# Column order of x2 in a transformer block's expert stage: contiguous chunks, and a straight gather for the second group

## The chip, the cores and the metric

The kernel runs on one core of a Trainium2 chip. The metric is the device time of one execution in microseconds. Of the kernel before three runs are known: 765.41 us in the median, 764.91 and 768.2 at the ends. All durations come from one further execution, taken by the hardware profiler.

## The reference, cut to what matters

An encoder block on 512 tokens of width 1024: attention of two kinds with one output projection into the residual stream, then a mixture of experts. The residual stream after attention is called x2 here. What the change touches:

```python
h2 = rms_norm(x, g_ffn[l])
pg = softmax(hf @ wg + bg); gsel = argmax(pg)            # one of 4 expert groups
p_top, e_loc = top_k(softmax(le[gsel]), 2)               # two of its 8 experts
gate = pg_sel[:, None] * p_top / sum(p_top)
ys = (silu(xb @ w1[e]) * (xb @ w3[e])) @ w2[e]           # each expert on its tokens
out[tok] += gate * ys                                    # x + out is returned
```

There are 32 experts; w1 and w3 are 1024 x 512 and w2 is 512 x 1024 for each, all in float32. Each token goes to two experts.

## The kernel before, in words

The first 260 us are attention and its output projection. Then x2 lies in SBUF (`xs`) as four tiles of 128 tokens (t = 0 to 3) by 1024 columns, worked on in two halves h of 512 columns.

**Router.** `half_turn` (line 800 on) transposes a half of a token tile by four TensorE transposes of 128 x 128 (line 808) into a bank of PSUM, and ACT copies it (`x2T`). `logits` multiplies it by the router's rows. DVE picks group and experts (`route`), TensorE counts tokens per expert (`count`), DVE makes the place of each token in its expert (`rank`) and, by `match` (line 919), a one-hot matrix that takes a token to a slot.

**Columns.** The contraction over 1024 columns runs in chunks of 128. Before, chunk r of half h is every fourth column, beginning with column r: column 4p + r of the half stands at partition p. Thus row p of the w1 and w3 loads is four neighbouring rows of the matrix, 8 KB in one piece, and x2 is read with a step of four elements. The router's rows and the gains g_ffn (`gfp`) follow the same order.

**Groups.** The experts are worked on in 13 groups, of two experts with 64 slots each or of four with 32 each. The order is (0,2), (2,2), (20,4), (4,2) and so on: first expert and number. For each group x2's rows are brought to the slots, transposed, in one of two ways:

- group 0: `gather_part` (line 922) multiplies x2 itself, as the stationary operand in float32, by the one-hot matrix: four matmuls (line 928) for each half and token tile, which give the transposed rows at once, in the two PSUM banks `px` (tag `tr`). One of these float32 matmuls stands in the trace as two records.
- groups 1 to 12: `prepare` (lines 1158 and 1159) splits a quarter of a half tile into two exact parts (`part`), a high one by a cast on ACT and the rest by a subtraction on DVE; `quarter` (line 1166) multiplies both by the one-hot matrix, 16 quarters a group; ACT copies the result (`st`, line 1172) and `turn` transposes it (line 1178).

`take` (line 1186) then scales by g_ffn on DVE. `finish` (line 1196) makes the turned one-hot matrix and the gates of a group. `hidden` (line 1224) multiplies the gathered rows by w1 and w3, `swish` and `gated` join them, `turn_hidden` (line 1263) transposes, `outputs` (line 1280) multiplies by w2, and `combine` (lines 1324 to 1326) adds the results back into `sums`.

**Order.** It is written out by hand. Group i's `hidden` has 16 steps; in step n, behind its matmuls, the functions in `during[n]` are issued: the previous group's `combine`, and the gathering of group i + 1. `outputs` has eight steps with `after[n]`, in which the gathering of group i + 2 begins. Group 0 is special: in its steps the experts are named (1), the places turned (3), its own last two gather parts done (4), the places sorted and group 1 begun (7); from step 8 on group 1's 16 quarters are issued, two a step, with a turn in step 13 and one behind the last step, and in step 11 group 0's `finish`.

**Loads.** Weights come in pieces of 1 MB on SP's queue (line 715), in the order of use, into a ring of tiles (`bt`, `qs`, `kl`, `kh`, `e`, `n`, `ma`, `mb`, `w_h`, `w_l`). A tile is loaded again when its last reader is done, and SP issues in order.

Of the kernel before, what the change touches and what calls it, by code (L numbers as in the profile page):

```python
# [22 lines left out]
P = 128  # L23
SEQ = 512
D = 1024
NT = SEQ // P
KC = D // P
NE = 32
HID = 512
# [53 lines left out]
def run(*gens):  # L83

    gens = list(gens)
    while gens:
        for g in list(gens):
            try:
                next(g)
            except StopIteration:  # L90
                gens.remove(g)
# [3 lines left out]
def tile_block(ctx: ExitStack, tc: tile.TileContext, a: dict, out: bass.AP):  # L95
    nc = tc.nc
# [6 lines left out]
    def bank(tag, shape=(P, 512), name=None):  # L103
        return psum.tile(list(shape), F32, tag=tag, name=name or f"ps_{tag}")
# [103 lines left out]
    ident = const.tile([P, P], F32, name="ident")  # L208
# [437 lines left out]
    for i, (g, n, j) in enumerate(ORDER):  # L646
        r = res[g, j]
# [1 line left out]
        wv.add(with_split(i, gen))  # L649


    w1 = a["w1"][0].rearrange("e (h p r) f -> e h p (r f)", h=2, p=P)
    w3 = a["w3"][0].rearrange("e (h p r) f -> e h p (r f)", h=2, p=P)
    w2 = a["w2"].rearrange("e c p q j d -> e c p (q j d)")
    NP = NE // 2

# [73 lines left out]
    x_tile = []  # L730
# [27 lines left out]
    gfp = const.tile([P, 2, 4], F32, name="gfp")  # L758
# [5 lines left out]
    iota_s = const.tile([P, SLOTS], F32, name="iota_s")  # L764

    def router_loads():
        nc.sync.dma_start(gfp, a["g_ffn"][0].rearrange("(h p r) -> p h r", h=2, p=P))
        raw_r = pool_at.tile([P, KC, 64], F32, tag="qn", name="raw_r", bufs=2)
        parts = {"w_router_g": raw_r[:, 0:1, 0:32], "w_router_e": raw_r[:, 1:5]}
        for n, r in (("w_router_g", 4), ("w_router_e", 32)):  # L770
            parts[n] = parts[n].rearrange("p a b -> p (a b)").rearrange("p (h c) -> p h c", h=2)
            nc.sync.dma_start(parts[n], a[n][0].rearrange("(h p r) c -> p h (r c)", h=2, p=P))
        for src, c0, n in ((a["b_router_g"], 0, 4), (a["b_router_e"], 4, 32)):
            nc.sync.dma_start(rbias[:, c0:c0 + n], bass.AP(tensor=src.tensor, offset=src.offset, ap=[[0, P], [1, n]]))
        nc.gpsimd.iota(desc, pattern=[[-1, 4]], base=4, channel_multiplier=0, allow_small_or_imprecise_dtypes=True)
        nc.gpsimd.iota(iota_s, pattern=[[1, SLOTS]], base=1, channel_multiplier=0,
                       allow_small_or_imprecise_dtypes=True)
        nc.gpsimd.iota(iota_e, pattern=[[1, NE]], base=0, channel_multiplier=0, allow_small_or_imprecise_dtypes=True)
        nc.gpsimd.affine_select(before, ones_f, pattern=[[1, P]], compare_op=ALU.is_gt, fill=0.0,
                                base=0, channel_multiplier=-1)  # L780
        nc.gpsimd.memset(ones_b, 1.0)
        nc.gpsimd.iota(favour, pattern=[[-1, NE]], base=NE - 1, channel_multiplier=0,
                       allow_small_or_imprecise_dtypes=True)
        nc.gpsimd.iota(favour[:, 0:FIXED], pattern=[[-1, FIXED]], base=FIXED, channel_multiplier=0,
                       allow_small_or_imprecise_dtypes=True)
        nc.gpsimd.tensor_scalar(favour[:, 0:FIXED], favour[:, 0:FIXED], 1e6, None, op0=ALU.mult)
        nc.gpsimd.iota(ids, pattern=[[0, 1]], base=0, channel_multiplier=1, allow_small_or_imprecise_dtypes=True)

        def gains():
            for n, c0, w in (("w_router_g", 0, 4), ("w_router_e", 4, 32)):  # L790
                nc.vector.tensor_tensor(wr[:, :, c0:c0 + w], parts[n].rearrange("p h (r c) -> p (h r) c", r=4),
                                        gfp.rearrange("p h r -> p (h r)").unsqueeze(2).to_broadcast([P, KC, w]),
                                        op=ALU.mult)

        wv.chain((12, gains))
# [6 lines left out]
    def half_turn(t, h, tag="tr"):  # L802

        xh = x_tile[0][:, t, h * 512:(h + 1) * 512]
        pb = bank(tag)
        xp = xh.rearrange("p (b r) -> p r b", r=4)
        for r in range(4):
            nc.tensor.transpose(pb[:, r * P:(r + 1) * P], xp[:, r], ident)
        x2T[2 * t + h] = pool_raw.tile([P, 4, P], F32, tag="w_raw", name="x2T", bufs=4)
        nc.scalar.copy(x2T[2 * t + h], pb.rearrange("p (k t) -> p k t", k=4))  # L810

# [110 lines left out]
    def gather_part(px, oh, h, ts_):  # L922

        for t in ts_:
            x2 = x_tile[0][:, t, h * 512:(h + 1) * 512].rearrange("p (b r) -> p r b", r=4)
            one = oh[:, t].rearrange("p e s -> p (e s)").bitcast(F32)
            for r in range(4):
                nc.tensor.matmul(px[h][:, r], lhsT=x2[:, r], rhs=one, start=(t == NT - 1 and r == 0),
                                 stop=(t == 0 and r == 3), skip_group_check=True)
# [206 lines left out]
    def dispatch(oh, p, px=None):  # L1136
# [6 lines left out]
        d = {"px": px, "parts": rows}  # L1143
# [8 lines left out]
        def prepare(n):  # L1152

            h, t, q = n // 8, NT - 1 - n // 2 % NT, n % 2
            part = d[n] = wk("part", [P, 2, 256], F32R, bufs=2)
            whole = x_tile[0][:, t, h * 512:(h + 1) * 512].rearrange("p (b r) -> p r b", r=4)[:, 2 * q:2 * q + 2]
            hi, lo = (part[:, m].rearrange("p (r b) -> p r b", r=2) for m in range(2))
            nc.scalar.copy(hi, whole)  # L1158
            nc.vector.tensor_tensor(lo, whole, hi.bitcast(F32), op=ALU.subtract)  # L1159

# [220 lines left out]
    def group_dispatch(i, oh=None, px=None):  # L1381
        first, n = groups[i]
        if oh is None:
            oh = one_hot((rank if first < FIXED else rank_s)[:, :, first:first + n], i == 1)
        return dispatch(oh, first // 2, px)

    d = group_dispatch(0, oh0, px)
# [5 lines left out]
    PAUSE = 7  # L1393

    def begin(i):
        d = following[i] = group_dispatch(i)
        d["prepare"](0), d["prepare"](1)

    def call(i, name, *args):
        following[i][name](*args)  # L1400
# [1 line left out]
    for i in range(NG):  # L1402
        last = i == NG - 1
        if i == 1:
            rounds = nc.values_load(cint[0:1, 0:1], min_val=0, max_val=7)
        if not last:
            rest = ahead if i == 0 else load_parts(i + 1)
            for nxt in islice(rest, 1) if i == PAUSE else rest:
                pass
        during, after = [[] for _ in range(16)], [[] for _ in range(8)]  # L1410
        if i == 0:
            def first_gather(d=d):
                d["gather"](1, (1, 0))
                d["take"](1)

            during[1] = [name_experts]
            during[3] = [turn_places]
            during[4] = [first_gather]
            during[7] = [sort_places, partial(begin, 1)]
            during[11] = [lambda d=d: run(d["finish"]("tr"))]  # L1420
        else:
            for n in range(8):
                at_ = (3 if n < 4 else 7) if last else 3 + n // 2 if i == PAUSE else 4 + n // 2 * 2
                during[at_].append(partial(combine, *prev, n // 4, (n % 4,), i == 1))
        if not last:
            if i == PAUSE:
                during[7] += [overflow, lambda: list(rest), partial(begin, i + 1)]
                work_on = [(8 + n // 2, "quarter", n) for n in range(16)] + [(13, "turn")]
            elif i + 1 in following and i:
                work_on = [(n // 2 * 2 - 4, "quarter", n) for n in range(4, 16)] + [(6, "turn")]  # L1430
            elif i:
                begin(i + 1)
                work_on = [(n * 12 // 16 + 2, "quarter", n) for n in range(16)] + [(10, "turn")]
            else:
                work_on = [(8 + n // 2, "quarter", n) for n in range(16)] + [(13, "turn")]
            for n, *what in work_on:
                during[n].append(partial(call, i + 1, *what))
        sl = hidden(i, tiles, d, during)
        if not last:
            call(i + 1, "turn")  # L1440
        ht = turn_hidden(sl, iter(()) if last else following[i + 1]["finish"]("o"))
        if last:
            break
        nd = following[i + 1]
        nd["take"](0), nd["take"](1)
        if i + 2 < NG and i + 1 != PAUSE:
            after[0].append(partial(begin, i + 2))
            for n in range(4):
                after[4 + n // 2 * 2].append(partial(call, i + 2, "quarter", n, "mm"))
        prev = outputs(tiles, ht, d, after), d["oht"]  # L1450
        tiles, d = nxt, following[i + 1]
# [85 lines left out]
```

## Time and profile before

| | |
|---|---|
| median of three runs | 765.41 us |
| profiled execution | 766.24 us |
| its span in the trace | 764.4 us |
| PE (TensorE) busy | 733.8 us, 96% |
| PEld (its weight loads) busy | 457.7 us, 60% |
| DVE busy | 440.3 us, 58% |
| ACT busy | 360.0 us, 47% |
| bytes moved | 228.84 MB, 299 GB/s in the mean |

The profiled execution's time exceeds its span by 1.84 us, which lies around the span. An engine's share of busy time is an average over stages with different limits: what a stage costs is read from that stage. Matmuls are pipelined, and the end of each is modelled, so the durations of neighbouring records overlap, and the pace of a series is read from its starts.

### The profile page before, as it was taken

How to read it: one execution, taken by the hardware profiler on the slowest of the kernel's cores; microseconds unless marked ns; L12 is line 12 of the kernel's file. 1: busy time of each engine (PE TensorE's matmuls, PEld its weight loads, DVE VectorE, ACT ScalarE, POOL GpSimd, SP SyncE). 2: the span in 40 equal slices, each digit the busy share in tenths (PEclk: the TensorE clock that was granted, in tenths of full speed). 3: DMA queues.
4: the chain of work that ended last, by engine and by line, in shares of the span. 5: the costliest groups of instructions: out<-in, count | busy, mean ns of one | idle time of the engine just before them, and what ended most of it. 6: DMA issues, size and time to landing. Idle time of an engine off the chain costs nothing. (4 is left out here: it accounts for less than half of the span.)

```text
span 764.4 us, 13043 instructions
## 1 busy us (share of the span) xinstructions
PE 733.8 (96%) x4748; PEld 457.7 (60%) x4748; DVE 440.3 (58%) x932; ACT 360.0 (47%) x725; POOL 91.8 (12%) x175
## 2 busy tenths in 40 slices
PE   9999999999999999899999999999789999999976
PEld 8899988977889895454444444443234444444223
DVE  4677778776765452565655656563455565565303
ACT  6575867877654421643543434341254344353000
POOL 0302100566663110000000000000000000000000
PEclk9999999999999999999999999999899999999999
DMA  8533111313664955557999999999999999999996
GB/s 312 161 113 91 56 56 55 126 42 111 197 254 172 409 232 208 198 216 316 419 421 420 422 421 419 422 421 419 418 421 421 421 420 420 423 421 420 416 409 258
DMA packets 45902, 228.84 MB, mean 299 GB/s; under 512 B 6885, under 2 KB 9189, under 8 KB 22921
## 3 DMA queue, kind: packets, MB, share of 16 engines
q1 hardware_dynamic: 45688, 227.96, 75.1%
q8 instruction: 38, 0.62, 0.3%
q14 instruction: 32, 0.25, 0.1%
q10 hardware_dynamic: 144, 0.00, 0.0%
HBM read 225.83 MB, written 2.11 MB: 298 GB/s over the span
## 5 line engine op out<-in xcount | busy, mean ns | idle before, releaser
L1158 ACT CAST part<-xs 128x256 fp32r<-128x256 f32 x192 | 119.9, 674 | 121.7 <-PE ps_mm L1166 43.0
L1159 DVE TENSOR_TENSOR part<-xs,part 128x256 fp32r<-128x256 f32 x192 | 115.9, 635 | 58.2 <-ACT part L1158 54.7
L1326 DVE TENSOR_TENSOR sums<-ps_o,sums 128x512 f32<-128x512 f32 x88 | 56.7, 686 | 45.7 <-PE ps_o L1325 45.7
L313 PE MATMUL ps_mm<-w_h,hTl 128*128 128x256 f32 x240 | 69.5, 290 | 0.2
L1224 PE MATMUL ps_mm<-qs,xt 128*64 128x512 f32 (+1 forms) x136 | 68.4, 615 | 1.1 <-DMA qs<-in_w 1.1
L313 PE MATMUL ps_mm<-w_h,hTh 128*128 128x256 f32 x240 | 67.3, 281 | 0.0
L313 PE MATMUL ps_mm<-w_l,hTh 128*128 128x256 f32 x240 | 67.3, 280 | 0.0
L1224 PE MATMUL ps_mm<-mb,xt 128*64 128x512 f32 (+1 forms) x120 | 59.8, 616 | 4.4 <-PEq L1341 4.4
L1224 PE MATMUL ps_mm<-kl,xt 128*64 128x512 f32 (+1 forms) x120 | 60.3, 616 | 0.0
L1224 PE MATMUL ps_mm<-kh,xt 128*64 128x512 f32 (+1 forms) x104 | 50.8, 601 | 0.2 <-DMA kh<-in_w 0.2
L1224 PE MATMUL ps_mm<-w_l,xt 128*64 128x512 f32 (+1 forms) x128 | 50.7, 602 | 0.0
L1224 PE MATMUL ps_mm<-w_h,xt 128*64 128x512 f32 (+1 forms) x120 | 46.8, 601 | 0.0
L313 PEld LDWEIGHTS ps_mm<-w_h,hTl 128*128 128x128 f32 x240 | 45.2, 189 | 1.1 <-DVE hTl L239 0.8
L180 DVE TENSOR_TENSOR w_l<-w_raw,w_h 128x512 fp32r<-128x512 f32 x64 | 44.4, 708 | 1.6 <-ACT w_h L177 1.4
L313 PEld LDWEIGHTS ps_mm<-w_l,hTh 128*128 128x128 f32 x240 | 45.3, 189 | 0.1
L313 PEld LDWEIGHTS ps_mm<-w_h,hTh 128*128 128x128 f32 x240 | 45.2, 188 | 0.0
L518 DVE TENSOR_TENSOR_SCAN p<-p,ones_f 128x513 f32<-128x513 f32 (+3 forms) x32 | 27.5, 859 | 30.6 <-POOL p L513 30.5
L1324 PE MATMUL ps_o<-yl,oht 128*128 128x512 f32 x96 | 43.2, 450 | 0.6 <-DVE sums L1326 0.6
L1253 DVE SCALAR_TENSOR_TENSOR sl<-ps_mm,rsl,sl 128x256 f32<-128x256 f32 x26 | 11.4, 479 | 54.9 <-PE ps_mm L1224 54.9
L1324 PEld LDWEIGHTS ps_o<-yl,oht 128*128 128x128 f32 x96 | 17.9, 187 | 41.8 <-DVE part L1159 24.4
L1267 ACT COPY sl<-ps_mm 128x256 f32<-128x256 f32 x26 | 10.0, 386 | 68.7 <-PE ps_mm L1263 68.7
L177 ACT CAST w_h<-w_raw 128x512 fp32r<-128x512 f32 x64 | 38.2, 621 | 5.2 <-DMA w_raw<-in_w_in 4.9
(299 smaller groups left out, 1781.2 us busy)
## 6 DMA issues: line engine op xcount, KB each, us to landing
qs<-in_w SPq DMA_DIRECT2D x22, 1024.0 KB, 19.8
e<-in_w SPq DMA_DIRECT2D x22, 1024.0 KB, 19.8
kl<-in_w SPq DMA_DIRECT2D x21, 1024.0 KB, 19.8
kh<-in_w SPq DMA_DIRECT2D x21, 1024.0 KB, 19.8
n<-in_w SPq DMA_DIRECT2D x20, 1024.0 KB, 19.8
mb<-in_w SPq DMA_DIRECT2D x20, 1024.0 KB, 19.8
w_h<-in_w SPq DMA_DIRECT2D x20, 1024.0 KB, 19.8
w_l<-in_w SPq DMA_DIRECT2D x20, 1024.0 KB, 19.8
```

Source lines behind the costliest of these rows:

```text
L177: nc.scalar.copy(part(wh, n), raw[i, n])
L180: eng.tensor_tensor(part(wl, n), raw[i, n], part(wh, n).bitcast(F32), op=ALU.subtract)
L313: nc.tensor.matmul(pb[:, u], lhsT=x(t0 + u, k), rhs=y[:, k], start=first, stop=last, skip_group_check=True)
L518: nc.vector.tensor_tensor_scan(rev, rev, ones_f[:, 0:1].to_broadcast([P, n + 1]), 1.0, op0=ALU.mult, op1=ALU.mult)
L1158: nc.scalar.copy(hi, whole)
L1159: nc.vector.tensor_tensor(lo, whole, hi.bitcast(F32), op=ALU.subtract)
L1224: nc.tensor.matmul(ph[n][part], lhsT=d["xt"][h][:, r, part], rhs=w, start=(h == 0 and r == 0), stop=(h == 1 and r == 3))
L1253: nc.vector.scalar_tensor_tensor(s, ph["w3"][:, c], d["rsl"], s, op0=ALU.mult, op1=ALU.mult)
L1267: nc.scalar.copy(s, pb)
L1324: nc.tensor.matmul(pc, lhsT=oht[:, t], rhs=yl[:, c], start=True, stop=False)
L1326: nc.vector.tensor_tensor(sums[0][:, t, cs], pc, (xs if first else sums[0])[:, t, cs], op=ALU.add)
```

## The change

The columns of a half are cut into four contiguous chunks of 128: chunk r of half h is columns 128r to 128r + 127 of it. The host lays out w1, w3, the router's rows and g_ffn to suit, so that the rows of a load remain in one piece for each partition; `half_turn`, `gather_part` and `prepare` read x2 contiguously. Group 1 is now gathered as group 0 is, by eight calls of `gather_part` in steps 8 to 15 of group 0, one a step; it has no `prepare`, `quarter` or `turn`. Its two `px` banks have the tag `tr`, and group 0's `finish` moves from `tr` to the tag `o`. Groups 2 to 12 keep the quarters.

```diff
-    w1 = a["w1"][0].rearrange("e (h p r) f -> e h p (r f)", h=2, p=P)
-    w3 = a["w3"][0].rearrange("e (h p r) f -> e h p (r f)", h=2, p=P)
+    w1, w3 = (a[n].rearrange("e h p r f -> e h p (r f)") for n in ("w1", "w3"))
...
-        nc.sync.dma_start(gfp, a["g_ffn"][0].rearrange("(h p r) -> p h r", h=2, p=P))
+        nc.sync.dma_start(gfp, a["g_ffn"])
...
-            nc.sync.dma_start(parts[n], a[n][0].rearrange("(h p r) c -> p h (r c)", h=2, p=P))
+            nc.sync.dma_start(parts[n], a[n].rearrange("p h r c -> p h (r c)"))
...
-        xp = xh.rearrange("p (b r) -> p r b", r=4)
         for r in range(4):
-            nc.tensor.transpose(pb[:, r * P:(r + 1) * P], xp[:, r], ident)
+            nc.tensor.transpose(pb[:, r * P:(r + 1) * P], xh[:, r * P:(r + 1) * P], ident)
...
-            x2 = x_tile[0][:, t, h * 512:(h + 1) * 512].rearrange("p (b r) -> p r b", r=4)
+            x2 = x_tile[0][:, t, h * 512:(h + 1) * 512].rearrange("p (r b) -> p r b", r=4)
...
-            whole = x_tile[0][:, t, h * 512:(h + 1) * 512].rearrange("p (b r) -> p r b", r=4)[:, 2 * q:2 * q + 2]
-            hi, lo = (part[:, m].rearrange("p (r b) -> p r b", r=2) for m in range(2))
+            whole = x_tile[0][:, t, h * 512 + q * 256:h * 512 + q * 256 + 256]
+            hi, lo = part[:, 0], part[:, 1]
...
     def begin(i):
         d = following[i] = group_dispatch(i)
-        d["prepare"](0), d["prepare"](1)
+        if i > 1:
+            d["prepare"](0), d["prepare"](1)
...
-            during[11] = [lambda d=d: run(d["finish"]("tr"))]
+            during[11] = [lambda d=d: run(d["finish"]("o"))]
...
-                work_on = [(8 + n // 2, "quarter", n) for n in range(16)] + [(13, "turn")]
+                work_on = [(8 + n, "gather", n // 4, (NT - 1 - n % 4,)) for n in range(8)]
...
-        if not last:
+        if not last and i:
             call(i + 1, "turn")
...
+    for n in ("w1", "w3"):
+        data[n] = np.ascontiguousarray(data[n][0].reshape(NE, 2, 4, P, HID).transpose(0, 1, 3, 2, 4))
+    for n in ("w_router_g", "w_router_e"):
+        data[n] = np.ascontiguousarray(data[n][0].reshape(2, 4, P, -1).transpose(2, 0, 1, 3))
+    data["g_ffn"] = np.ascontiguousarray(data["g_ffn"][0].reshape(2, 4, P).transpose(2, 0, 1))
```

## Rows read from the trace of the kernel before

**Rows 1.** Stages: window and length; busy time (instructions) by engine; PEclk, DMA share, GB/s.

```profile
275.30:287.66 12.36, 11.80 (x59) 11.63 (x60) 4.52 (x33) 0.31 (x2) 2.63 (x8) 1.00 0.44 173
287.66:302.14 14.48, 14.48 (x76) 8.44 (x77) 2.68 (x17) 1.05 (x2) 0.00 (x0) 1.00 0.44 155
302.14:324.00 21.86, 17.86 (x85) 8.44 (x84) 11.86 (x26) 13.93 (x26) 0.00 (x0) 1.00 0.58 223
324.00:356.00 32.00, 32.00 (x161) 15.39 (x161) 19.00 (x37) 13.72 (x25) 0.00 (x0) 1.00 0.60 235
356.00:755.00 399.00, 384.31 (x2108) 166.55 (x2107) 214.02 (x416) 149.33 (x273) 0.00 (x0) 0.99 1.01 418
```

**Rows 2.** The chain that ended last: start, length, what.

```profile
744.87 10.08 DMA qs<-in_w
```

**Rows 3.** Waits of the load queue, 280 to 362 us: total, times, longest.

```profile
SPq L715 <- PE ps_mm L1224: 49.0, 7, 11.9
```

**Rows 4.** Weight loads by source line: duration ns min/median/max, first and last start.

```profile
L928 PEld LDWEIGHTS ps_tr<-oh,xs x64: 308/329/332, 275.3 to 297.1; 128*128 128x128 f32 x64
...
L220 PEld LDWEIGHTS ps_sc<-ones_f x6: 190/192/192, 737.8 to 738.4; 128*128 128x128 f32 x6
...
L808 PEld LDWEIGHTS ps_tr<-ident,xs x24: 195/209/218, 260.7 to 271.4; 128*128 128x128 f32 x24
...
L1178 PEld LDWEIGHTS ps_tr<-ident,st x96: 138/140/143, 317.1 to 701.3; 128*128 128x128 f32 x96
```

**Rows 5.** TensorE's timeline, 275 to 298 us.

```profile
275.35 5.84 PE L928 MATMUL ps_tr<-oh,xs 128*128 128x128 f32 x24 [0.29 <-DVE oh L919]
281.02 0.20 PE L909 MATMUL ps_o<-act,ones_b 128*128 128x32 bf16 x2
...
281.30 5.84 PE L928 MATMUL ps_tr<-oh,xs 128*128 128x128 f32 x24
287.66 0.64 PE L1224 MATMUL ps_mm<-bt,xt 128*64 128x512 f32 x1 [0.52 <-DVE xt L1186]
...
293.59 4.00 PE L928 MATMUL ps_tr<-oh,xs 128*128 128x128 f32 x16
```

**Rows 6.** TensorE's timeline, contiguous f32 matmuls: start, length of the series, count.

```profile
92.47 0.88 PE L607 MATMUL ps_o<-v,pT 128*128 128x128 f32 x6
...
737.95 0.83 PE L220 MATMUL ps_sc<-ones_f 128*128 128x128 f32 x6
```

**Rows 7.** DVE's timeline: act, the second one-hot, group 1's one-hot.

```profile
277.54 0.41 DVE L882 SCALAR_TENSOR_TENSOR act<-iota_e,idx,a 128x32 bf16<-128x32 f32 x2
...
281.75 0.43 DVE L919 TENSOR_TENSOR oh<-rank,iota_s 128x256 fp32r<-128x256 f32 x1
...
303.05 0.69 DVE L919 TENSOR_TENSOR oht<-rank,iota_s 128x512 fp32r<-128x512 f32 x1
```

**Rows 8.** POOL's timeline: its last instruction on the router's tiles.

```profile
284.51 0.34 POOL L1067 TENSOR_TENSOR book<-rstd,book 128x64 fp32r<-128x64 f32 x1
```

**Rows 9.** TensorE's groups, 302.14 to 324 us: busy, mean ns, idle before.

```profile
L1166 PE MATMUL ps_sc<-part,oht 128*128 128x256 f32 x32 | 7.4, 324 | 3.3 <-DVE part L1159 3.2
...
L1178 PE MATMUL ps_tr<-ident,st 128*128 128x128 f32 x8 | 1.3, 279 | 0.7 <-ACT st L1172 0.7
```

**Rows 10.** TensorE's timeline in the same stage: its first step, a late pair, an undelayed one.

```profile
302.14 1.08 PE L1224 MATMUL ps_mm<-e,xt 128*64 128x512 f32 x4
304.31 1.02 PE L1166 MATMUL ps_sc<-part,oht 128*128 128x256 f32 x4 [1.09 <-DVE part L1159]
...
318.77 0.74 PE L1166 MATMUL ps_sc<-part,oht 128*128 128x256 f32 x4
319.44 0.64 PE L1224 MATMUL ps_mm<-qs,xt 128*64 128x512 f32 x1
```

**Rows 11.** Page, part 5: busy, mean ns, idle before.

```profile
L1158 ACT CAST part<-xs 128x256 fp32r<-128x256 f32 x192 | 119.9, 674 | 121.7 <-PE ps_mm L1166 43.0
...
L1267 ACT COPY sl<-ps_mm 128x256 f32<-128x256 f32 x26 | 10.0, 386 | 68.7 <-PE ps_mm L1263 68.7
```

## The prediction

> **What bounds the kernel now.** I read the stages first [rows 1]. From 356 us to 755 us the DMA share is 1.01 and the rate 418 GB/s: the expert weights stream without a gap, and TensorE, though 384 of 399 us busy, only follows. Between 275 and 356 us the share is 0.44, 0.44, 0.58 and 0.60, because the weight tiles form a ring and a tile is loaded again only when the matmul that reads it is done. The chain of waits ends as this suggests: its last long piece is a weight transfer, landing at 754.95 [rows 2]. The queue's own waits [rows 3] name what holds the loads back in 280 to 362 us: hidden products of TensorE, 49.0 us in 7 waits. So the stream is fixed in length (the bytes stay the same) and its start follows TensorE's order of work through groups 0 and 1. A microsecond that TensorE gains between the last router work (260 us) and the first hidden step of group 2 (after 356 us) starts the full stream a microsecond earlier and ends the run a microsecond earlier. What ACT or DVE gain behind 356 us is worth nothing, as the transfers cover it.
>
> **What the new column order changes for a matmul.** Before, x2 is the stationary operand with a step of four elements. The loads of 128 columns [rows 4] take 329 ns in the gather (L928) against 192 ns for a contiguous f32 operand of the same shape (L220), and 209 against 140 ns in transposes (L808, L1178). The gather is limited by this: PEld is busy 11.63 of 12.36 us in its stage [rows 1], and 24 records take 5.84 us, 0.243 us each [rows 5]. A contiguous f32 matmul of 128 by 128 by 128 goes at (0.83-0.275)/5 = 0.111 us (L220) or (0.88-0.275)/5 = 0.121 us (L607) a record, 0.275 being the last one's own length [rows 6]. I take 0.115, so each record gains 0.128 us; the bounds are 0.111 and, if the step is not the cause, 0.243. One gather part (one token tile, one half) is four matmuls of two records each: eight records, 1.94 us now and 0.92 us after.
>
> A rule of the Trainium skill speaks against this: "TensorE: Matmul & The Clock Gate", section "LDWEIGHTS (loading the stationary operand)", gives the load by its column count alone (columns over 1.2, in ns), whatever the layout. By it no record would get shorter, which is the slower case below; the loads in rows 4 have 128 columns each and still differ, so the trace does not agree.
>
> **Transposes before the router.** There are 32 transposes of x2. Those that the critical path sees are the 16 of token tiles 3 and 2, ahead of their logits. With 69 ns less per load [rows 4] they give between 0 (load hidden) and 1.1 us; I take 0.4. The other 16 lie beside DVE's routing of tiles 3 and 2, so they give nothing.
>
> **Group 0's gather: before its first hidden product.** Now: three parts from 275.35, the counts from 281.02, then one part and the last two from 281.30 to 287.14, the scaling by DVE, the first hidden product at 287.66 [rows 5]. After: the first three parts take 24 x 0.115 = 2.76 us and end 277.7 (with the 0.4 above). The counts need DVE's act, written by 277.95 now [rows 7], 277.55 then, so they start at once where they now wait for TensorE. The second one-hot was ready at 282.18, 1.16 us after the counts [rows 7]; after, it is ready at 278.9, when the part that covers it ends. Two more parts, 1.84 us, and the same 0.5 us for the scaling give 281.3. Gain: 48 x 0.128 = 6.1, less 0.1 for the wait on act: 6.0 us. A possible new wait is here. POOL's last instruction on the router's tiles ends at 284.85 [rows 8], 3.8 us behind the counts, so at 281.5 after; if DVE's scaled tile takes over memory that POOL still reads, it waits 0 to 0.8 us, and behind it every hidden product. I take 0 and keep 0.8 for the range.
>
> **Group 0's last two parts.** They lie between hidden products from 293.59 [rows 5]: 16 x 0.128 = 2.0 us.
>
> **Group 1: quarters out, straight gather in.** This is the stage 302.14 to 324.00 us, in which TensorE is busy 17.86 of 21.86 us [rows 1]. Removed: 4.0 us of idle time, which is almost all waits of the quarter products for DVE's halves (3.2) and of the turns for ACT (0.7) [rows 9]; 8 pairs of quarters, at least 0.67 us each by the starts of a pair that waits for nothing [rows 10], 5.4, and at most the 7.4 us busy; two turns of four transposes, at most 1.3 and some 0.8 us. So 10.2 to 12.7 us; I take 11.5, since most pairs also wait inside. Added: eight parts, 64 x 0.115 = 7.4 us, and one wait. The gather needs the one-hot of group 1, which DVE writes from 303.05 for 0.69 us [rows 7]; TensorE's step begins at 302.14 and is done at 303.22, so it waits some 0.5 us (0 to the 1.09 until 304.31 that it waits there now [rows 10]), and behind it stand all hidden steps of group 0. Net 11.5 - 7.4 - 0.5 = 3.6 us; with the ends of the pace too, 1.4 and 5.6.
>
> Edits that I cost at nothing. Group 0's finish moves to the other pair of banks, last read by ACT and DVE at the sorting, some 8 us before it is written. The banks that the new gather takes were emptied by DVE before that sorting. The 16 casts and subtractions dropped free ACT and DVE, which nobody waits for then, and the table load of the activation no longer stands in a queue of casts. In later groups a cast of 128 by 256 takes 674 ns; a contiguous copy of that size takes 386 [rows 11]. That is up to 0.29 us in each of 176 casts, some 50 us of ACT, and the like on DVE, all under the stream. Without that cover it would save TensorE its waits for halves, which after 324 us are near nil (32.00 of 32.00 busy) [rows 1]. The w1 and w3 transfers keep their 8 KB per partition in one piece and their order. The six small router loads go out by 202 us and are used after 260; a microsecond more or less on SP is covered.
>
> **The sum.** 0.4 + 6.0 + 2.0 + 3.6 = 12.0 us. Against the profiled execution's own 766.24 us (span 764.4 and 1.84 around it) that is 754.2; against the median of 765.41, 753.4. I put down 753.8. What is late next: the stream itself, saturated from about 344 us, with TensorE's work on groups 1 and 2 unchanged behind it.
>
> **The rivals.**
> 1. *The pace does not follow the layout* (slower). If a record of f32 gather stays at 0.243 us, group 0 gains nothing and group 1 pays 64 x 0.243 = 15.6 + 0.5 for the 11.5 removed: 4.6 us slower, 770.0 us by the median. The place is the eight new parts between group 0's hidden products. It decides from the record pace at which 128 records in all cost what is saved: (64 x 0.243 + 11.5 + 0.4 - 0.6)/128 = 0.21 us. For it: the added matmuls are f32 and two records each, where quarters were one. Against it: rows 4 and 6.
> 2. *Only group 0 gains.* The halves' waits are replaced by others of the same size (the one-hot, a bank, POOL's 0.8), so that group 1's swap gives 0 to 1: 765.4 - 8 + 1 = 758 to 759. For it: 0.5 us of DVE's work is already late there. Against it: ACT and DVE lose 32 instructions of 0.6 us in this stage.
> 3. *Hidden anyway.* If the full stream does not start earlier, since some load of group 2 is held by something that does not move, the end stays at 765 to 766. For it: DMA is at 1.01 in half of the run. Against it: shares under 0.6 before 356 and waits that name TensorE.
>
> **How the numbers follow.** Forecast 0.74 (its own range 750.3 to 757.1: with every term at its better end 1.1 + 6.3 + 2.1 + 5.6 = 15.1 us, at its poorer end 0 + 5.0 + 1.9 + 1.4 = 8.3, from the median); rival 2 0.13; rival 3 0.06; rival 1 0.05; more than the best ends 0.02. The range 750.5 to 760 leaves out rivals 1 and 3 and little else. About 0.5%, 3.8 us, is what this kernel's measurement can tell from none: faster 0.89 (forecast, rival 2, more), the same 0.06, slower 0.05.
>
> **What would show it.** The loads of L928 at about 190 ns and 0.11 to 0.12 us a record; 128 of these records instead of 64; the first hidden product at about 281.3 us; TensorE's wait for L1159 gone before group 0's output products, and those starting at about 312; the share at 1.01 from about 344 to 743. The prediction is wrong if the gather's records stay near 0.24 us, if group 0's output products start later than 316, or if the stream starts at 344 and then shows gaps.

## The result, and the profile after

The changed kernel takes 754.62 us in the median of four runs (754.32 to 755.27), the kernel before 766.36 in four runs beside them: a ratio of 0.9847, 95% interval 0.9821 to 0.9872. The forecast was 753.8 us, with a range of 750.5 to 760. The profiled execution took 755.27 us with a span of 753.6, so 10.8 us of span went; by the medians it is 11.7.

The stages of the changed kernel, as in [rows 1]: window and length; busy time (instructions) of PE, PEld, DVE, ACT, POOL; granted clock, DMA share, GB/s.

```profile
275.18:281.71 6.53, 6.01 (x60) 5.81 (x60) 4.49 (x33) 0.31 (x2) 2.57 (x8) 1.00 0.63 261
281.71:294.24 12.53, 12.53 (x77) 6.49 (x77) 2.68 (x17) 1.05 (x2) 0.04 (x1) 1.00 0.65 222
294.24:313.12 18.88, 18.31 (x109) 10.67 (x108) 2.81 (x10) 3.53 (x8) 0.00 (x0) 1.00 0.59 224
313.12:345.10 31.98, 31.98 (x162) 15.37 (x161) 15.26 (x37) 9.53 (x25) 0.00 (x0) 1.00 0.64 255
345.10:744.20 399.10, 386.16 (x2109) 168.95 (x2107) 175.52 (x416) 106.48 (x273) 0.00 (x0) 0.98 1.01 418
```

The first four windows begin at the same events as before: first gather, first hidden product, step 8 of group 0, first output product. The first three lost 5.8, 2.0 and 3.0 us. The last window begins 32 us behind the output product and ends 9.4 us ahead of the span's end, in both kernels, so its equal length only repeats that these two events lie as far apart as before. What it adds is that the DMA share is 1.01 again, though ACT and DVE are 43 and 38.5 us less busy.

TensorE's timeline after, from the gather to the first output product, which answers to [rows 5]:

```profile
275.18 2.92 PE L926 MATMUL ps_tr<-oh,xs 128*128 128x128 f32 x24 [0.28 <-DVE oh L917]
...
278.21 2.98 PE L926 MATMUL ps_tr<-oh,xs 128*128 128x128 f32 x24
281.71 0.64 PE L1222 MATMUL ps_mm<-bt,xt 128*64 128x512 f32 x1 [0.52 <-DVE xt L1184]
...
287.63 2.05 PE L926 MATMUL ps_tr<-oh,xs 128*128 128x128 f32 x16
...
294.24 1.08 PE L1222 MATMUL ps_mm<-e,xt 128*64 128x512 f32 x4
295.89 1.16 PE L926 MATMUL ps_tr<-oht,xs 128*128 128x128 f32 x8 [0.57 <-DVE oht L917]
296.98 1.08 PE L1222 MATMUL ps_mm<-e,xt 128*64 128x512 f32 x4
297.99 1.16 PE L926 MATMUL ps_tr<-oht,xs 128*128 128x128 f32 x8
...
313.12 0.64 PE L1278 MATMUL ps_sc<-kh,sl 128*64 128x512 f32 x1
```

The same 24 records take 2.92 us where they took 5.84: (2.92 - 0.275)/23 = 0.115 us a record. The row at 295.89 shows the new wait for group 1's one-hot, 0.57 us. The rows from 296.98 on show a hidden step and a gather part in turn: 2.09 us for the two.

The weight loads by source line, after, which answer to [rows 4] (duration in ns, min/median/max):

```profile
L926 PEld LDWEIGHTS ps_tr<-oh,xs x64: 186/192/192, 275.1 to 289.3; 128*128 128x128 f32 x64
L926 PEld LDWEIGHTS ps_tr<-oht,xs x64: 186/192/192, 295.9 to 311.8; 128*128 128x128 f32 x64
...
L806 PEld LDWEIGHTS ps_tr<-ident,xs x24: 137/141/145, 260.9 to 271.4; 128*128 128x128 f32 x24
```

They fell from 329 to 192 and from 209 to 141 ns, the durations of the contiguous loads in rows 4. And the costliest groups of ACT and DVE after, from part 5 of the page (busy us, mean ns, idle before), which answer to [rows 11]:

```profile
L1156 ACT CAST part<-xs 128x256 fp32r<-128x256 f32 x176 | 63.1, 407 | 145.3 <-PE ps_mm L1164 58.8
L1157 DVE TENSOR_TENSOR part<-xs,part 128x256 fp32r<-128x256 f32 x176 | 66.8, 421 | 57.3 <-ACT part L1156 57.1
```

### The profile page after: what moved, and what is told of

It reads as the page before. It is cut to its first block, busy times and chain, and to the rows that moved or that the text cites. A ratio compares the mean times of both kernels' runs of the same rounds, so it can differ in the third digit from the quotient of the medians.

```text
span 753.6 us, 13045 instructions
## 1 busy us (share of the span) xinstructions
PE 728.4 (97%) x4772; PEld 455.0 (60%) x4772; DVE 389.0 (52%) x916; ACT 302.3 (40%) x707; POOL 92.3 (12%) x175
## 5 line engine op out<-in xcount | busy, mean ns | idle before, releaser
L1156 ACT CAST part<-xs 128x256 fp32r<-128x256 f32 x176 | 63.1, 407 | 145.3 <-PE ps_mm L1164 58.8
L1157 DVE TENSOR_TENSOR part<-xs,part 128x256 fp32r<-128x256 f32 x176 | 66.8, 421 | 57.3 <-ACT part L1156 57.1
L1164 PEld LDWEIGHTS ps_mm<-part,oh 128*128 128x128 f32 x160 | 21.8, 191 | 32.6 <-DVE part L1157 20.3
L1271 ACT ACTIVATE yh<-ps_sc,gsl 128x512 fp32r<-128x512 f32 (+1 forms) x28 | 18.3, 657 | 55.5 <-PE ps_sc L1278 55.5
```

The costliest lines, as they stand in the source:

```text
L1164: nc.tensor.matmul(d["rows"][:, q * 256:q * 256 + 256], lhsT=ohs[t], rhs=d[n][:, m], start=(n % 8 == 0 and m == 1), stop=(n % 8 == 7 and m ...
L1271: nc.scalar.activation(yh, py, AF.Copy, scale=gsl)
```

## The experiments

The time of the first output product of group 0 turned out to be the best ruler. From it to the end of the span it is 440.4 us before and 440.5 after; in the other profiles without a filler it is 440.2 to 440.6. Below, "stage" is the time from step 8 of group 0 to that product, and "lead" the time from the first hidden product to it: 36.34 us before, 31.41 after. Where a kernel starts a microsecond earlier or later in attention, which no edit here touches, these differences leave it out.

**The layout alone.** In the changed kernel, group 1 goes back to the quarters:

```diff
-        if i > 1:
-            d["prepare"](0), d["prepare"](1)
+        d["prepare"](0), d["prepare"](1)
...
-                work_on = [(8 + n, "gather", n // 4, (NT - 1 - n % 4,)) for n in range(8)]
+                work_on = [(8 + n // 2, "quarter", n) for n in range(16)] + [(13, "turn")]
```

with the finish back in `tr` and the turn for every group.

> The contiguous columns alone; group 1 is gathered by 16 quarters and two turns again. Theory (two separate gains): the layout gives what the stages up to 294 us gave, 0.2 + 5.8 + 2.0 = 8.0 us, and the stage from group 0's step 8 to its output products stays at 21.9 us, so the time is 3.0 us above the changed kernel, 757.6. Rival (the layout also ends the waits of the quarters): a cast now takes 0.405 instead of 0.657 us and a subtraction 0.420 instead of 0.630, so most of the 3.2 us that TensorE waited for the halves goes by itself, the stage takes 19.0 to 19.5, and the time is 754.8 to 755.4; then the straight gather of group 1 is worth under 1 us.

Measured: 756.25 us (four runs), ratio to before 0.985 (0.9817 to 0.9883), span 753.8. Its stage, and its groups of instructions there (busy us, mean ns, idle before):

```profile
294.19:313.43 19.24, 16.48 (x85) 8.25 (x84) 8.72 (x26) 9.95 (x26) 0.00 (x0) 1.00 0.62 240
```

```profile
L1164 PE MATMUL ps_sc<-part,oht 128*128 128x256 f32 x32 | 6.1, 313 | 2.1 <-DVE part L1157 2.0
L1157 DVE TENSOR_TENSOR part<-xs,part 128x256 fp32r<-128x256 f32 x16 | 6.1, 421 | 6.9 <-ACT part L1156 6.9
L1156 ACT CAST part<-xs 128x256 fp32r<-128x256 f32 x16 | 5.7, 406 | 5.8 <-PE ps_sc L1164 5.8
...
L1176 PE MATMUL ps_tr<-ident,st 128*128 128x128 f32 x8 | 1.3, 279 | 0.7 <-ACT st L1170 0.7
```

The casts and subtractions of this stage in the kernel before, from 302.14 to 324.00 us:

```profile
L1158 ACT CAST part<-xs 128x256 fp32r<-128x256 f32 x16 | 9.7, 657 | 4.6 <-PE ps_sc L1166 4.6
L1159 DVE TENSOR_TENSOR part<-xs,part 128x256 fp32r<-128x256 f32 x16 | 9.3, 616 | 6.8 <-ACT part L1158 6.8
```

The rival holds. With the layout the quarters' stage falls from 21.86 to 19.24 us by itself: the wait for DVE's halves goes from 3.2 [rows 9] to 2.0 us, and the pairs, which also wait inside, from 7.4 to 6.1. Casts and subtractions, the only instructions of this stage that read x2, are what became shorter: 657 to 406 ns and 616 to 421 ns. The straight gather then adds 19.24 - 18.88 = 0.36 us.

**The swap alone.** The kernel before, with group 1's gather straight and the step of four left in:

```diff
-                work_on = [(8 + n // 2, "quarter", n) for n in range(16)] + [(13, "turn")]
+                work_on = [(8 + n, "gather", n // 4, (NT - 1 - n % 4,)) for n in range(8)]
```

and the three small edits that go with it.

> The kernel before with group 1's straight gather alone, columns with the step of four. Theory (the step sets the pace of the f32 records): 64 more records at 0.243 us, so the stage takes 18.9 + 64 x 0.128 = 27.1 us instead of 21.9, 5.2 us slower than before, 770.6 to 771.6. Rival (the pace comes from something else, such as the place of the gather among other work): the added records run at 0.12 and the stage takes 18.9, 3 us faster than before, 763.

Measured: 771.74 us (ten runs) against 767.69 before, ratio 1.0049 (1.0031 to 1.0066). Its stage, and the loads of the added records:

```profile
303.88:330.56 26.68, 26.11 (x110) 18.46 (x109) 2.81 (x10) 3.53 (x8) 0.00 (x0) 1.00 0.46 176
```

```profile
L928 PEld LDWEIGHTS ps_tr<-oht,xs x64: 307/329/332, 305.5 to 329.1; 128*128 128x128 f32 x64
```

The stage is 4.8 us longer than before, where 5.2 was expected. So the step is the cause of the pace, and the forecast's first rival describes the swap without the layout.

**A filler on either side.** Twenty f32 matmuls of 128 by 128 by 128 that nobody reads, added to the changed kernel in step 9 of group 0 or in step 1 of group 8:

```diff
+        if i == 0:
+            during[9].append(partial(keep_clock, 20, "o"))
```

(the other has `i == 8` and `during[1]`).

> The changed kernel with 20 added f32 matmuls of 128 by 128 by 128 (40 records of 0.115 us, 4.6 to 4.9 us of TensorE) in step 9 of group 0. Theory (the stream of weights starts when TensorE lets it): the whole shift reaches the end, 754.6 + 4.7 = 759.3. Rival (the loads of that stage are held by something else): less than half of it, under 757.

> The changed kernel with the same 20 matmuls in step 1 of group 8, in the middle of the saturated stream. Theory: TensorE only follows there, so nothing reaches the end, 754.3 to 755.3. Rival (TensorE, 97% busy, is the bound throughout): 4.7 us reach the end, 759.3.

Measured: 759.3 us early and 756.0 late, ratios 0.9887 (0.9856 to 0.9918) and 0.9847 (0.9813 to 0.9881). The two fillers in their kernels' timelines of TensorE:

```profile
298.62 4.63 PE L220 MATMUL ps_o<-ones_f 128*128 128x128 f32 x40
```

```profile
571.85 4.73 PE L220 MATMUL ps_o<-ones_f 128*128 128x128 f32 x40
```

Early, the lead grows from 31.41 to 35.89 us (281.34 to 317.23), and from there to the end it is 440.3 again: all of the 4.5 us reach the end. Late, the time from the first output product to the end is 440.9 instead of 440.5: of 4.7 us some 0.4 reach it. The late kernel's profiled execution (756.36 us) is longer than the changed kernel's because its stage took 20.47 us instead of 18.88 (see the last section); for its other executions that isn't shown. So TensorE sets the start of the stream and not its length, though it is 97% busy.

**The casts alone.** In the changed kernel `prepare` reads x2 with the step of four:

```diff
-            whole = x_tile[0][:, t, h * 512 + q * 256:h * 512 + q * 256 + 256]
-            hi, lo = part[:, 0], part[:, 1]
+            whole = x_tile[0][:, t, h * 512:(h + 1) * 512].rearrange("p (b r) -> p r b", r=4)[:, 2 * q:2 * q + 2]
+            hi, lo = (part[:, m].rearrange("p (r b) -> p r b", r=2) for m in range(2))
```

> The changed kernel, in which only the casts and subtractions of groups 2 to 12 read x2 with the step of four again (the quarters then get permuted columns, which changes the output of those groups but no instruction's size). Theory (behind group 0's output products the stream of weights sets the time): ACT and DVE are some 45 us busier in the sum, and from group 0's first output product to the end it stays 440.4 us; the time is that of the changed kernel within 0.5. Rival (the cheaper casts help TensorE in the later groups too): 1 to 3 us slower.

Measured: 756.28 us, ratio 0.9837 (0.9804 to 0.9869), span 755.0. Its costliest groups of ACT and DVE:

```profile
L1156 ACT CAST part<-xs 128x256 fp32r<-128x256 f32 x176 | 110.4, 678 | 117.0 <-PE ps_mm L1164 43.0 <-DVE sums L1324 39.1 <-PE ps_sc L1164 19.5
L1157 DVE TENSOR_TENSOR part<-xs,part 128x256 fp32r<-128x256 f32 x176 | 107.0, 639 | 51.4 <-ACT part L1156 47.9
```

ACT is 47 and DVE 40 us busier in these groups, and from the first output product (314.62) to the end it takes 440.4 us, as expected. The span's 1.4 us over the changed kernel lie in the stage ahead (20.47 instead of 18.88 us), in which this edit changes no instruction; the last section says what they are. The median alone would have looked like a point for the rival.

**The one-hot first, and the gather in one block.**

```diff
-            during[7] = [sort_places, partial(begin, 1)]
+            during[7] = [partial(begin, 1), sort_places]
```

> The changed kernel with group 1 begun (its one-hot made by DVE) ahead of the sorting of places in step 7. Theory (TensorE's 0.57 us of wait for that one-hot in step 8 is on the path): the wait goes, and the time is 0.5 to 0.6 us lower. Rival (DVE then writes the sorted ranks later and something else waits): no change.

```diff
-                work_on = [(8 + n, "gather", n // 4, (NT - 1 - n % 4,)) for n in range(8)]
+                work_on = [(9, "gather", n // 4, (NT - 1 - n % 4,)) for n in range(8)]
```

> The changed kernel with all eight gather parts of group 1 in step 9 of group 0 instead of one in each of the steps 8 to 15. A hidden step and a gather part take 2.09 us together now; hidden steps on end take 0.86 to 0.91 and 24 records on end 2.76 to 2.92, 0.92 a part. Theory (each change between the two kinds of matmul costs TensorE some 0.15 us): seven steps save 0.3 us each, the stage is 1.8 to 2.3 us shorter, and so is the time, 2.0 under the changed kernel. Rival (the 0.3 us is the records' own cost): no change. The first two tiles read in step 11 come free 7 us later, which costs nothing if those loads are not late.

> Both: group 1 begun ahead of the sorting, and its eight gather parts in one block in step 8. Theory: the two gains add up, 2.6 us under the changed kernel, and the stage from step 8 to the output products takes some 16.2 instead of 18.9 us. Rival: the block waits for something else, and the gain is under 1.

Measured: 753.79 us with the one-hot first (753.67 to 753.96, ratio 0.9815, 0.9787 to 0.9843), 753.08 with the block (0.9808, 0.978 to 0.9835), 753.16 with both (0.981, 0.978 to 0.984). By the lead: 30.78, 29.58 and 29.58 us against 31.41. The first gained 0.63 us and the second 1.83, both near the expected time; the sum did not come, for the block in step 9 leaves DVE a second hidden step in which to write the one-hot, so that wait was gone already. TensorE's timeline with the one-hot first:

```profile
294.52 1.16 PE L926 MATMUL ps_tr<-oht,xs 128*128 128x128 f32 x8
```

With the block in step 9:

```profile
295.44 7.41 PE L926 MATMUL ps_tr<-oht,xs 128*128 128x128 f32 x64
...
309.75 0.41 PE L1261 MATMUL ps_mm<-ident,sl 128*128 128x128 f32 x2 [0.35 <-DVE sl L1251]
```

With both edits, the block now in step 8:

```profile
295.39 7.41 PE L926 MATMUL ps_tr<-oht,xs 128*128 128x128 f32 x64
302.73 2.80 PE L1222 MATMUL ps_mm<-e,xt 128*64 128x512 f32 x12
...
310.56 0.41 PE L1261 MATMUL ps_mm<-ident,sl 128*128 128x128 f32 x2 [0.35 <-DVE sl L1251]
```

64 records now take 7.41 us, 0.115 each, and three hidden steps 2.72. The last row is a new wait of 0.35 us: without a gather part behind the last hidden step, TensorE waits for DVE's gated rows. So the 1.83 us of the block are not all of the kind that its theory named: 0.57 is the one-hot's wait, gone with it, and 0.35 is lost to the new one, which leaves 1.83 - 0.57 + 0.35 = 1.6 us for fewer changes between the two kinds of matmul. Both edits against the one-hot first, neither of which has the one-hot's wait, give the same: 30.78 - 29.58 + 0.35 = 1.55. Why a change costs TensorE time is not shown.

**Side by side, and the block at the end.** Four kernels with five rounds on one chip: the changed one, the layout alone, the block in step 9, and the block behind the last hidden step:

```diff
-                work_on = [(8 + n, "gather", n // 4, (NT - 1 - n % 4,)) for n in range(8)]
+                work_on = [(15, "gather", n // 4, (NT - 1 - n % 4,)) for n in range(8)]
```

> The changed kernel again, beside the others of this call: 754.3 to 756.5, 1.5% under the kernel before.

> The contiguous columns alone, group 1 with quarters, as in the first experiment, now timed beside the changed kernel. Its stage from step 8 to the first output product was 19.24 us against 18.88, so it should be 0.3 to 0.4 us slower than the changed kernel, too little to tell apart; if the straight gather were worth the 3.0 us of that stage, it would be 3.0 slower.

> All eight gather parts in step 9, timed beside the changed kernel: the stage from the first hidden product to the first output product was 29.58 us against 31.41, so 1.8 us faster than the changed kernel; no gain if the earlier difference was one of chips.

> All eight gather parts behind the last hidden step (15) instead of step 9. Theory: one change between kinds of matmul less, and the block covers the 0.35 us in which TensorE waited for DVE's gated rows before the turns; the stage from the first hidden to the first output product takes 28.9 to 29.2 us, 0.4 to 0.7 faster than with the block in step 9. Rival (DVE scales group 1's rows too late, and group 0's output steps or group 1's hidden steps wait for it): no gain or up to 1 us slower.

| kernel | median us | ratio to before (95%) |
|---|---|---|
| changed | 756.73 | 0.9854 (0.983 to 0.9878) |
| layout alone | 757.94 | 0.9873 (0.9849 to 0.9897) |
| block in step 9 | 753.01 | 0.982 (0.9798 to 0.9841) |
| block in step 15 | 752.40 | 0.9805 (0.9784 to 0.9825) |

Before is 766.87 there. One of the changed kernel's five executions took 3847 us, which nothing recorded explains; the ratio leaves it out, and the median of the other four is 756.5. By either figure the changed kernel came out at or just above the top of its expected range. The block in step 9 lies 3.7 us under it by the medians, where 1.8 was expected; the changed kernel's profile here has a lead of 32.99 us instead of 31.41, 3.4 above the block's 29.58 (the last section says why). The intervals of neighbours overlap, so the order of the block's two places stands on the traces: the lead of the last kernel is 28.70 us (282.96 to 311.66), a little better than expected and 2.7 under the changed kernel's 31.41, and from there to the end it takes 440.6. In TensorE's timeline the block stands behind the last hidden step and the wait for the gated rows is gone:

```profile
303.33 7.41 PE L926 MATMUL ps_tr<-oht,xs 128*128 128x128 f32 x64
310.50 0.48 PE L1194 MATMUL ps_o<-book,oht 128*128 128x256 f32 x2
310.82 0.38 PE L1261 MATMUL ps_mm<-ident,sl 128*128 128x128 f32 x2
```

It has the shortest lead and the lowest median of all versions that were run, though the times alone do not tell it from the block in step 9.

## Why the prediction was right, and where not

The changed kernel's 754.62 us lie 0.8 above the forecast, in its own range. Term by term, by the starts of the same instructions in the two traces:

| term | forecast us | measured us |
|---|---|---|
| transposes: from the first of them to the first gather | 0.4 | 0.4 (14.37 to 14.00) |
| group 0's gather: from it to the first hidden product | 6.0 | 5.8 (12.31 to 6.53) |
| its last two parts: from there to step 8 | 2.0 | 2.0 (14.48 to 12.53) |
| group 1's stage: from there to the first output product | 3.6 | 3.0 (21.86 to 18.88) |

The sum is 11.1 where the forecast had 12.0; 0.2 us were lost ahead of the transposes, where nothing was changed, and the first output product came 10.9 us earlier, the end of the span 10.8.

*What bounds it* was right: the two fillers show it, and the constant 440 us.

*The pace of the gather* was right to the third digit (0.115 us). That digit is luck, since the rows it was taken from gave 0.111 and 0.121. The rule of the Trainium skill ("TensorE: Matmul & The Clock Gate", "LDWEIGHTS (loading the stationary operand)") that columns alone set the load disagrees with the loads above, 329 and 192 ns for the same 128 columns. The swap alone shows the cause: the same records take 329 ns a load with the step of four.

*Transposes*: the size was right, not the place, so its fit is luck. From the first transpose to the logits of tiles 3 and 2 only 0.14 us went (7.61 to 7.47). The rest came behind, from the other 16 transposes, which I had given nothing: the counts stand behind their logits in TensorE's order.

*POOL's possible wait* did not come: POOL's last instruction on the router's tiles ended at 281.75, and DVE wrote the scaled tile from 281.23 on.

*Group 1's stage* is the term that was mis-sized, by 0.6 us. A gather part between hidden steps takes up to 1.09 us and not the 0.92 of a series, and the eight together 8.4 by their starts instead of 7.4; the block shows it, with some 1.6 us gained by changing between the two kinds of matmul fewer times. The wait for the one-hot, 0.5 by forecast, was 0.57. By difference, what was taken out came to some 12.0 us instead of 11.5, which made up for half of the miss.

*What the stage was put down to* was wrong, though the sum hides it, since it sets the whole stage before against the whole stage after. I gave its 3.6 us to the straight gather and the cheaper casts nothing but cover behind the stream. The layout alone shows the reverse: 2.6 of the 3.0 us come from cheaper halves in the quarters' own stage, where TensorE did wait for them, and the straight gather is worth 0.4 once the layout is there and minus 4.8 where it is not. Behind 324 us before, the casts were worth nothing, as forecast.

*A slip in rival 2*: its 758 to 759 us do not follow from its condition. Group 0's terms of 8.4 us and a gain of 0 to 1 in group 1 give 756 to 757 from the median.

## What to carry to other kernels

Two edits in one change are not two gains: price each with the other already in place, since both may remove the same wait. When a transfer stream has a fixed length and full rate, find the event that starts it and measure to that event in each trace; a difference of a few tenths is then plain where medians of whole runs scatter by a microsecond or two. Here a gather part cost up to 1.09 us between hidden steps and 0.92 in a series, so it is worth trying gathers in one block, placed where it covers a wait.

## What the runs showed of the hardware

The clock. In the stage of step 8 the granted clock of TensorE fell in some profiles. The changed kernel, profiled a second time, shows it (PE, PEld, DVE, ACT, POOL, then clock):

```profile
294.00:296.00 2.00, 1.43 (x8) 0.51 (x8) 1.12 (x3) 0.34 (x1) 0.00 (x0) 1.00 1.02 406
296.00:298.00 2.00, 2.00 (x10) 1.58 (x12) 0.00 (x0) 0.00 (x0) 0.00 (x0) 0.58 1.02 426
298.00:300.00 2.00, 2.00 (x8) 0.59 (x5) 0.00 (x0) 0.00 (x0) 0.00 (x0) 0.57 0.45 180
300.00:302.00 2.00, 2.00 (x14) 1.07 (x13) 0.00 (x0) 0.00 (x0) 0.00 (x0) 1.00 0.03 12
```

A mean of 0.57 is mostly the lower level, 1.2 GHz, with some of 2.4; the late filler's profile has two microseconds at the lower level alone:

```profile
296.00:298.00 2.00, 2.00 (x7) 0.63 (x6) 0.00 (x0) 0.00 (x0) 0.00 (x0) 0.50 1.03 438
```

Just before, TensorE had 16 records of 32 columns, one hidden step and then, in the changed kernel, the wait of 0.57 us for the one-hot. The price is the lead: 32.99 us here against 31.41 in the first profile, 1.6 us (1.4 in the layout alone, 33.17 against 31.77). The fall is in four of the eight profiles of edited kernels in which TensorE waits in step 8 (this one, one of the two of the layout alone, the late filler, the strided casts) and in none of the five in which it does not (one-hot first, both profiles of the block in step 9, the two other blocks). The kernel before waited 1.09 us there and kept its clock in its one profile. So the wait may be the cause, but 14 profiles are too few to show it. It is one source of the scatter between executions and not the only one: the kernels without the wait scatter by 0.3 (one-hot first) to 2.4 us (the block in step 9), and their profiles differ by up to 2 us in when the router begins, ahead of all that the change touches.
